# A hybrid decoder layer on one core: x in three token pieces, attention scores as three one-pass products, y split two tiles ahead

## The chip, the core and the metric

The kernel runs on one core of a Trainium2 chip. The time is the device time of one launch in microseconds; the kernel before was run three times, and the median stands for it. A separate, profiled execution left the trace that all views here come from. Engines: PE is TensorE's matrix product and PEld its weight load, DVE is VectorE, ACT is ScalarE, POOL is GpSimd, SP issues transfers.

## The reference

One decoder layer over 16 meta tokens and 1024 tokens (1040 positions), width 1024. Two mixers read the same normalised x; their outputs go through W_out, and a gated convolution FFN follows.

```python
xn = rms_norm(h, mix_pre_g[l])
proj = xn @ w_in[l]                       # z, xbc, dt, q, k, v
y_ssd = ssd_mixer(z, xbc, dt_raw, ...)
y_sb = rms_norm(stick_breaking_attention(q, k, v).reshape(Bsz, L, SB_WIDTH), sb_norm_g[l])
mix = jnp.concatenate([y_ssd, y_sb], axis=-1) @ w_out[l]
h = h + rms_norm(mix, mix_post_g[l])
# then h = h + rms_norm(ffn(rms_norm(h)))
```

The attention has 16 heads of 64. For a query t and an earlier key s the weight is beta[t,s] times the product of (1 - beta[t,j]) over the keys j between, with beta = sigmoid(q.k/8).

## The kernel before, in words

**Products in split precision.** Most float32 products are made of three one-pass products of type float32r: an operand a is split into a high part ah (a rounded) and a low part al = a - ah, and ah*bh + al*bh + ah*bl is summed in one PSUM bank. ScalarE makes the high part, GpSimd or VectorE the low part. Products of plain float32 operands appear in the trace as two records each.

**Stages.** x is normalised, transposed and split into `xh` and `xl` (L197 to L283). The SSD mixer follows (to 415 us of the trace), then the attention (415 to about 981 us), then W_out's second half with the norms, then the FFN's up and down products. W_out's first half takes the SSD output and is done inside the attention.

**Projections.** `project_steps` (L154) multiplies one 1024 x 128 weight block, split by `load_w`, with all tokens in the three chunks of `CH`: 348, 346 and 346 columns, 24 products each, into a bank of tag "mm" of which there are two. It yields after each chunk, or also half-way through one where `halves_` is set. `qkv_steps` (L353) makes q, k and v of one pair of heads p (0 to 7) so: nine steps for pair 0, fifteen for pair 1, eighteen for the others. Steps of all pairs in a row, with the transposes of v behind each pair, form `fill` (L661). Twelve of its 135 steps run in the SSD stage.

**Attention.** The loop at L897 goes through 8 pairs of heads and 8 query blocks of 128; a block is written (p,i). TensorE's order there is the program's order (L896); a planner of the framework orders the other engines, from dependencies, program order and modelled costs. Each block does in turn:

- `block_weights` (L682): scores `z` of the block against n = 16 + 128(i+1) keys, in chunks of up to 512 keys (144; 272; 400; two of 264, 328, 392, 456; three of 348, 348, 344). q and k are float32; the two heads of the pair lie on partitions 0 to 63 and 64 to 127. ScalarE takes two sigmoids of each chunk, VectorE scans each head (L704), GpSimd multiplies (L706). Scores and transposes share two double banks, tag "zz". For i = 7 the third chunk comes only after the next item.
- `run(fill, 1 + (i < 3))` (L905): one or two projection steps.
- `block_mix` (L726): the weights of an earlier block times v, `av`, in two column halves.
- `block_turn` (L710): transposes `tw` of the weights of the block two before; ScalarE copies them out as `th`.
- one more projection step (L914).

At i = 3 `edge_mix` (L750) of the pair before stands between scores and projection. From the counts of L905 and L914, pairs 1 to 5 use 19 steps each, and `fill` is used up in (6,4).

**W_out's first half.** After `fill` has ended (L915), the pool of x is closed and a pool of its own is opened in its place. `wout_steps` (L813) takes the eight 128-row blocks of W_out: the raw block (loaded ahead from (6,4), L907), the high part on ScalarE, the low part on VectorE (L828), and small products for the two halo rows (L820) into one of the two "mm" banks. Four blocks are prepared in (6,5), four in (6,6). `ssd_half` (L876) then multiplies the eight token tiles of y with W_out, two steps of 24 products per tile: one step in (6,7), in pair 7 at i = 1, 3, 5, 6, 7, and the rest behind the attention. The y of tile t+1 is loaded and split (`split_y`, L853: transfer, ScalarE, GpSimd) when tile t begins. Behind the attention its raw tile comes from the pool `est` (L961), which is opened there.

Of the kernel before, what the change touches and what calls it, by code (L numbers as in the profile page):

```python
# [8 lines left out]
F32 = mybir.dt.float32  # L9
# [22 lines left out]
CH = [(0, 348), (348, 346), (694, 346)]  # L32
# [19 lines left out]
def tile_layer(ctx: ExitStack, tc: tile.TileContext, x, meta, rows, parts,  # L52
# [101 lines left out]
    def project_steps(w, ncol, xh, xl, chunks, evac, name, halves_=False):  # L154
        hi, lo = w
        for c0, n in chunks:
            acc = psum_mm(f"pj_{name}_{c0}")
            for k in range(KB):
                if halves_ and k == KB // 2:
                    yield  # L160
                for j, (a, b) in enumerate(((hi, xh), (hi, xl), (lo, xh))):
                    mm(acc[:ncol, :n], a[:, k, :ncol], b[:, k, c0:c0 + n],
                       start=(k == 0 and j == 0), stop=(k == KB - 1 and j == 2))
# [33 lines left out]
    xh = xp.tile([P, KB, L], F32R, name="xh", tag="xh")  # L197
    xl = xp.tile([P, KB, L], F32R, name="xl", tag="xl")

    def conv_chain(b, nm, w, halves_=False):  # L200
# [5 lines left out]

        return raw, project_steps(w, P, xh, xl, CH, ev, nm, halves_)

    dtT = rp.tile([32, L + 3], F32, name="dtT", tag="rt", bufs=1)

    def dt_steps(hl):
        for c0, n in CH:
            acc = psum_mm(f"pj_dt_{c0}")
            for k in range(KB):
                for j, src in enumerate((xh, xl)):
                    mm(acc[:32, :n], hl[:, k, :], src[:, k, c0:c0 + n],
                       start=(k == 0 and j == 0), stop=(k == KB - 1 and j == 1))
# [4 lines left out]
    with tc.tile_pool(name="pre", bufs=3, side="right") as pre, \  # L222
# [46 lines left out]
        def turn_x(i):  # L269
            c0, nr = spans[i]  # L270
            tps = []
            for hf in range(2):
# [6 lines left out]
                tps.append((tp, (slice(None), slice(4 * hf, 4 * hf + 4), slice(c0, c0 + nr))))  # L279
            for tp, dst in tps:  # L280
                nc.scalar.activation(xh[dst], tp[:, :, :nr], AF.Copy)
            for tp, dst in tps:
                nc.vector.tensor_tensor(xl[dst], tp[:, :, :nr], xh[dst].bitcast(F32), op=ALU.subtract)  # L283
# [62 lines left out]
    def qkv_block(name, evac, halves_):  # L346
        w = weights_of(name)
        for i, _ in enumerate(project_steps(w, P, xh, xl, CH, evac, name, halves_)):
# [3 lines left out]

    def qkv_steps(p, post):  # L353
        q = rp.tile([P, L + 3], F32, tag="rq", name=f"q{p}", bufs=3)
        k = rp.tile([P, L], F32, tag="rk", name=f"k{p}", bufs=3)
        for dst, nm in ((q, "q"), (k, "k")):
            def ev(acc, c0, n, dst=dst):
                nc.scalar.activation(dst[:, c0:c0 + n], acc[:, :n], AF.Copy)

            yield from qkv_block(f"{nm}{p}", ev, p > 1 or (p, nm) == (1, "k"))  # L360
        vt = rp.tile([P, L], F32, tag="rt", name=f"vt{p}", bufs=1)

        def evv(acc, c0, n):
            nc.scalar.activation(vt[:, c0:c0 + n], acc[:, :n], AF.Copy)

        v = rp.tile([P, NT + 1, P], F32, tag="rv", name=f"v{p}")
        vc = rp.tile([P, P], F32, tag="vc", name=f"vc{p}")
        heads[p] = q, k, v, vc
        yield from qkv_block(f"v{p}", evv, p > 0)

        def turn_v(part):
            tp = psum_tp(f"vtp{p}_{part}")
# [5 lines left out]
        def turn_edge():  # L378
            edge = rp.tile([P, NT, NM], F32, tag="edge", name=f"edge{p}", bufs=1)
# [7 lines left out]
            nc.vector.tensor_copy(meta_k[:, p, :], k[:, 0:NM])  # L387
# [20 lines left out]
    with tc.tile_pool(name="ssd", bufs=1, side="right") as sp:  # L408
# [49 lines left out]
        def z_steps(g, b):  # L458
# [5 lines left out]
            yield from project_steps(load_w(w_z[4 * g + b], P, f"z{g}{b}"), P, xh, xl, CH, evz, f"z{g}{b}")  # L464
# [216 lines left out]

    def block_weights(p, i):  # L682
        q, k = heads[p][:2]
        nm = f"{p}_{i}"
        if i == 0:
            edges[p] = ap.tile([P, 2, NT, NM], F32, tag="cb", name=f"cb{p}", bufs=2)
            nc.gpsimd.memset(edges[p][:, :, :, NM - 1:], 0.0)
        t0, n = NM + i * P, NM + (i + 1) * P
# [4 lines left out]
        for ci, (a, w) in enumerate(chunks):  # L693
# [3 lines left out]
            for j in range(2):  # L697
                h = halves[j]
                mm(z[:, j, :w], q[h, t0:t0 + P], k[h, a:a + w], start=True, stop=True)  # L699
            nc.scalar.activation(kp[:, :, a:a + w], z[:, :, :w], AF.Sigmoid, scale=-QSCALE)  # L700
            nc.scalar.activation(bt[:, :, a:a + w], z[:, :, :w], AF.Sigmoid, scale=QSCALE)  # L701
        m = n - NM
# [110 lines left out]
    def wout_steps(pool, half, gain, res, y0, acc, raws_):  # L813
# [930 lines left out]
```

## Time and profile before

| | us |
|---|---|
| median of 3 runs | 1810.53 |
| lowest, highest | 1805.03, 1811.18 |
| profiled execution, whole | 1805.86 |
| its span, first to last instruction | 1804.2 |
| attention, from the first scores | 415.2 |
| attention, store of the last pair's output | 981.7 |

In a view of windows a row holds the stretch, its length, then for each engine the busy time and the number of records, the granted clock of TensorE (1.00 is full), the share of the transfer engines in use, and GB/s. In a timeline a row holds start, length (up to the last end of what was merged), engine, line, operation, output and inputs, shapes and count; records of TensorE overlap, so that the time of one is read from one start to the next. In the groups, the number behind the bar is the busy time, then the mean of one in ns, then the idle time of the engine ahead of them with what ended it. In a view of waits: total, times, longest.

### The profile page before, as it was taken

The numbers are of one execution on the slowest core, as the hardware profiler recorded it, in microseconds if no ns is written. First come the engines' busy times: TensorE is split into PE (matmuls) and PEld (weight loads), VectorE is DVE, ScalarE is ACT, GpSimd is POOL, SyncE is SP. The second block draws the span as 40 slices with busy tenths as digits, with TensorE's granted clock in tenths as the row PEclk, the third lists the DMA queues.
The fourth block names the chain that finished last, engine by engine and source line by source line (L and its number), as shares of the span: only waits on it lengthen the run. The fifth ranks groups of instructions, "written<-read, shape, count | busy, mean of one in ns | idle before, by whom it ended". The sixth has DMA issues, their size and how long they took to land. (4 is left out here: it accounts for less than half of the span.)

```text
span 1804.2 us, 27314 instructions
## 1 busy us (share of the span) xinstructions
PE 1732.4 (96%) x10942; PEld 1487.3 (82%) x10942; DVE 1061.6 (59%) x1125; ACT 830.8 (46%) x1373; POOL 867.8 (48%) x615
## 2 busy tenths in 40 slices
PE   6999999999999999999799899899999999999997
PEld 6899889888888888886567588888999988888886
DVE  5651964873463454355741256666766666657988
ACT  5423553645565565566653333543333333244444
POOL 4223753676555564554751223277777776600001
PEclk9999999999999999999999899999999999999999
DMA  4133333231011011012212545222333332196344
GB/s 157 48 97 106 106 118 107 71 94 36 24 37 48 24 36 37 24 48 71 72 42 95 193 140 164 82 88 88 117 100 106 101 105 88 64 320 227 95 123 158
DMA packets 90547, 173.96 MB, mean 96 GB/s; under 512 B 10698, under 2 KB 35818, under 8 KB 90420
## 3 DMA queue, kind: packets, MB, share of 16 engines
q1 hardware_dynamic: 90420, 172.21, 30.0%
q8 instruction: 86, 1.41, 0.3%
q14 instruction: 41, 0.34, 0.1%
HBM read 122.39 MB, written 49.79 MB: 95 GB/s over the span
## 5 line engine op out<-in xcount | busy, mean ns | idle before, releaser
L704 DVE TENSOR_TENSOR_SCAN kp<-kp,hold 128x272 f32<-128x272 f32 (+7 forms) x128 | 207.8, 1665 | 193.5 <-ACT kp L700 103.2
L706 POOL TENSOR_TENSOR bt<-bt,kp 128x256 f32<-128x256 f32 (+7 forms) x128 | 214.7, 1695 | 188.9 <-DVE kp L704 132.7
L1109 POOL TENSOR_TENSOR wl<-wr,wh 128x1024 fp32r<-128x1024 f32 x44 | 110.7, 2524 | 40.7 <-ACT wh L1108 40.7
L1557 PE MATMUL dn<-dl,dh 128*128 128x512 f32 x308 | 119.9, 389 | 0.1
L1557 PE MATMUL dn<-dh 128*128 128x512 f32 x308 | 119.9, 389 | 0.0
L1557 PE MATMUL dn<-dh,dl 128*128 128x512 f32 x308 | 119.8, 389 | 0.0
L1603 POOL TENSOR_TENSOR fms<-fms,nhalf 128x1 f32<-128x1 f32 x8 | 8.5, 1060 | 225.7 <-DMA ar<-fda 186.0
L700 ACT ACTIVATE kp<-z 128x288 f32<-128x288 f32 (+6 forms) x112 | 82.8, 739 | 56.7 <-PE z L699 33.0
L1486 ACT ACTIVATE dh<-ar 128x512 fp32r<-128x512 f32 x77 | 48.7, 632 | 111.3 <-PE dn L1557 90.7
L699 PE MATMUL z<-k,q 64*128 64x144 f32 (+6 forms) x448 | 86.9, 487 | 13.3 <-ACT bt L701 6.0
L1108 ACT ACTIVATE wh<-wr 128x1024 fp32r<-128x1024 f32 x44 | 46.6, 1060 | 114.7 <-PE fX L1166 68.3
L1238 DVE SCALAR_TENSOR_TENSOR ga<-gr,pp,ga 128x1024 f32<-128x1024 f32 x44 | 71.4, 1622 | 34.8 <-ACT ga L1231 34.0
L722 ACT ACTIVATE th<-tw 128x1024 f32<-128x1024 f32 (+2 forms) x96 | 74.7, 813 | 34.1 <-PE tw L720 32.2
L701 ACT ACTIVATE bt<-z 128x288 f32<-128x288 f32 (+6 forms) x112 | 83.1, 742 | 0.0
L720 PE MATMUL tw<-ident,bt 128*128 128x128 f32 x576 | 77.6, 280 | 3.8 <-issue 2.8
L734 PEld LDWEIGHTS av<-th,v 128*64 128x64 f32 x1152 | 62.6, 138 | 18.9 <-issue 17.9
L734 PE MATMUL av<-th,v 128*64 128x128 f32 x1152 | 78.0, 281 | 0.0
L1487 DVE TENSOR_TENSOR dl<-ar,dh 128x512 fp32r<-128x512 f32 x77 | 53.2, 691 | 41.7 <-ACT dh L1486 41.7
L720 PEld LDWEIGHTS tw<-ident,bt 128*128 128x128 f32 x576 | 62.1, 141 | 15.5 <-issue 12.9
L699 PEld LDWEIGHTS z<-k,q 64*128 64x128 f32 x448 | 36.7, 186 | 41.8 <-issue 18.5
L1557 PEld LDWEIGHTS dn<-dl,dh 128*128 128x128 f32 x308 | 57.8, 188 | 12.5 <-DVE dl L1487 0.4
L1557 PEld LDWEIGHTS dn<-dh 128*128 128x128 f32 x308 | 57.8, 188 | 12.4 <-ACT dh L1486 0.3
(550 smaller groups left out, 5752.6 us busy)
## 6 DMA issues: line engine op xcount, KB each, us to landing
wr<-in_w_up SPq DMA_DIRECT2D x44, 512.0 KB
fds<-ga SPq DMA_DIRECT2D x44, 256.0 KB
b<-in_w_down SPq DMA_DIRECT2D x44, 256.0 KB
ar<-fds SPq DMA_DIRECT2D x44, 256.0 KB
fda<-ga SPq DMA_DIRECT2D x33, 256.0 KB
ar<-fda SPq DMA_DIRECT2D x33, 256.0 KB
yk<-yd SPq DMA_DIRECT2D x16, 512.0 KB
zd<-zt SPq DMA_DIRECT2D x8, 520.0 KB
```

The costliest lines, as they stand in the source:

```text
L699: mm(z[:, j, :w], q[h, t0:t0 + P], k[h, a:a + w], start=True, stop=True)
L700: nc.scalar.activation(kp[:, :, a:a + w], z[:, :, :w], AF.Sigmoid, scale=-QSCALE)
L701: nc.scalar.activation(bt[:, :, a:a + w], z[:, :, :w], AF.Sigmoid, scale=QSCALE)
L704: nc.vector.tensor_tensor_scan(kp[:, j][:, ::-1], kp[:, j][:, ::-1], hold[:, L - n:L][:, ::-1], 0.0, op0=ALU.mult, op1=ALU.max)
L706: nc.gpsimd.tensor_tensor(bt[:, j, 0:m], bt[:, j, 0:m], kp[:, j, 1:m + 1], op=ALU.mult)
L720: nc.tensor.transpose(tw[:, j, b, :], bt[:, j, c0:c0 + P], ident)
L722: nc.scalar.activation(th[:, :, :nb, :], tw[:, :, :nb, :], AF.Copy)
L734: mm(av[halves[j], :], v[:, kb, halves[j]], th[:, j, b, :], start=kb == 0, stop=kb == i)
L1109: nc.gpsimd.tensor_tensor(l, raw, h.bitcast(F32), op=ALU.subtract)
L1238: nc.vector.scalar_tensor_tensor(v, self.g[jj][:, :, i:i + 256], fconv_w[:, j, i:i + 1], v, op0=ALU.mult, op1=ALU.add)
L1487: sub(lo[:, k], raw, hi[:, k].bitcast(F32), op=ALU.subtract)
L1557: mm(banks[t], u[:, 0, c], v[:, 1, :], start=(p == 0 and i == 0), stop=(p == NPR - 1 and i == 2))
```

## The change

x is kept as three tiles (`xs`), one for each chunk of tokens (400, 384, 256 columns), each with its high and low part. The projections of pair 7 go through the chunks one by one, q, k and v of each, so that a tile of x is free after its chunk. W_out's first half is put into these tiles: three blocks in the first, three in the second, two in the third (`third_slots`), one block for each attention block from (6,2) to (7,1), with its raw loads issued there. The halo accumulator is taken at (6,2).

The scores become three float32r products for each head. k is split where it leaves PSUM (`kh` on ScalarE, `kl` on VectorE), q block by block, one block ahead (`split_q`, on VectorE). The values `av` come straight behind the scores. One projection step per block goes (`FILL`), so that pairs 2 to 6 use 17 steps. The products of W_out's first half run one step per block from (7,2).

`ssd_half` splits the y of tile t+2 when tile t begins; two are split ahead of the first.

```diff
-CH = [(0, 348), (348, 346), (694, 346)]
+CH = [(0, 400), (400, 384), (784, 256)]
...
-                for j, (a, b) in enumerate(((hi, xh), (hi, xl), (lo, xh))):
-                    mm(acc[:ncol, :n], a[:, k, :ncol], b[:, k, c0:c0 + n],
+                for j, (a, b) in enumerate(((hi, 0), (hi, 1), (lo, 0))):
+                    mm(acc[:ncol, :n], a[:, k, :ncol], xs[c0][:, b, k, :n],
...
-    xh = xp.tile([P, KB, L], F32R, name="xh", tag="xh")
-    xl = xp.tile([P, KB, L], F32R, name="xl", tag="xl")
+    def x_third(c0, name):
+        n = dict(CH)[c0]
+        return xp.tile([P, 2, KB, n], F32R, name=name, tag=f"x{c0}")
+
+    xs = {c0: x_third(c0, f"xs{c0}") for c0, _ in CH}
...
+        def ev_k(acc, c0, n):
+            if c0 == 0:
+                low_k()
+            kl = later["kl"]
+            nc.scalar.activation(kh[:, c0:c0 + n], acc[:, :n], AF.Copy)
+            nc.vector.tensor_tensor(kl[:, c0:c0 + n], acc[:, :n], kh[:, c0:c0 + n].bitcast(F32), op=ALU.subtract)
...
+        names = [(f"q{p}", ev_q), (f"k{p}", ev_k), (f"v{p}", ev_v)]
+        if p < 7:
+            for nm, ev in names:
+                yield from qkv_block(nm, ev, p > 1 or (p == 1 and nm != "q1"))
+        else:
+            for c in CH:
+                for j, (nm, ev) in enumerate(names):
+                    w = weights_of(nm)
+                    for i, _ in enumerate(project_steps(w, P, [c], ev, nm, True)):
+                        if i == 1 and c[0] == 0:
+                            weights_of(nm, 1)
+                        yield
+                left[0] += 1
...
-            nc.vector.tensor_copy(meta_k[:, p, :], k[:, 0:NM])
+            nc.vector.tensor_tensor(meta_k[:, p, :], kh[:, 0:NM].bitcast(F32), kl[:, 0:NM].bitcast(F32), op=ALU.add)
...
+    def split_q(p, i):
+        q = heads[p][0][:, NM + i * P:NM + (i + 1) * P]
+        qh = rp.tile([P, P], F32R, tag="qh", name=f"qh{p}_{i}", bufs=2)
+        ql = rp.tile([P, P], F32R, tag="ql", name=f"ql{p}_{i}", bufs=2)
+        nc.vector.tensor_copy(qh, q)
+        nc.vector.tensor_tensor(ql, q, qh.bitcast(F32), op=ALU.subtract)
+        qsplit[p, i] = qh, ql
...
-            for j in range(2):
-                h = halves[j]
-                mm(z[:, j, :w], q[h, t0:t0 + P], k[h, a:a + w], start=True, stop=True)
+            for s_, (u, r) in enumerate(((qh, kh), (ql, kh), (qh, kl))):
+                for h, j in zip(halves, range(2)):
+                    mm(z[:, j, :w], u[h, :], r[h, a:a + w], start=s_ == 0, stop=s_ == 2)
...
+        nxt = (p, i + 1) if i < NT - 1 else (p + 1, 0)
+        if nxt[0] in heads:
+            split_q(*nxt)
...
+    def third_slots():
+        free = []
+
+        def slots(k, nm):
+            if not free:
+                c0 = CH[k // 3][0]
+                flat = x_third(c0, f"wo{nm}{c0}").rearrange("p a b c -> p (a b c)")
+                free.extend(flat[:, o * D:(o + 1) * D] for o in range(2 * dict(CH)[c0] // P))
+            return free.pop(0), free.pop(0)
+
+        return slots
...
-            if t < NT:
-                ys.append(split_y(wp, 0, t + 1, ("whi", "wlo", WB)))
             y = ys.pop(0)
+            if t < NT - 1:
+                ys.append(split_y(wp, 0, t + 2, ("whi", "wlo", WB)))
...
+    FILL = (3, 2, 1, 1, 1, 1, 1, 0)
+    STAGE = {(6, 2): 1, (6, 3): 2, (6, 4): 3, (6, 5): 4, (6, 6): 5, (6, 7): 6, (7, 0): 7, (7, 1): 8}
...
             next(block, None)
+            if mix:
+                block_mix(*mix.pop(0))
             if p > 0 and i == 3:
                 edge_mix(p - 1, edge)
-            run(fill, 1 + (i < 3))
...
+            run(fill, 1 + (i < FILL[p]))
             run(block)
-            if mix:
-                block_mix(*mix.pop(0))
             if len(turn) > 2:
                 mix.append(block_turn(*turn.pop(0)))
             run(fill, int(p > 0 or i > 3))
...
+            if left[0] and wsteps is None:
+                wres = []
+                halo = psum_mm("halo0")
+                wsteps = wout_steps(third_slots(), 0, ssd_g, wres, halo_y(ap, 0, ssd_g), halo, [])
+            for _ in range(2):
+                if wsteps and len(wres) < min(8, 3 * left[0], STAGE.get((p, i), 0)):
+                    run(wsteps, 1)
+            if wsteps and first is None and len(wres) == 8:
+                run(wsteps)
+                halo_store(ap, 0, halo)
+                ys1 = [split_y(wp, 0, t, ("whi", "wlo", WB)) for t in (1, 2)]
+                first = ssd_half(wres, ys1)
+            elif first:
+                run(first, 1)
```

More of the change, by code (lines that the diff above doesn't have):

```diff
@@ L152, in load_w, with project_steps @@
         return hi, lo
[L154 removed]
+    def project_steps(w, ncol, chunks, evac, name, halves_=False):
         hi, lo = w
@@ L351, in qkv_block @@
             yield
+    left = [0]
     def qkv_steps(p, post):
         q = rp.tile([P, L + 3], F32, tag="rq", name=f"q{p}", bufs=3)
[L355 to L369, printed above, removed]
+        kh = rp.tile([P, L], F32R, tag="rk", name=f"kh{p}", bufs=3)
+        later, vt_ = {}, []
+        def values():
+            v = rp.tile([P, NT + 1, P], F32, tag="rv", name=f"v{p}")
+            vc = rp.tile([P, P], F32, tag="vc", name=f"vc{p}")
+            heads[p][2:] = [v, vc]
@@ L371, in turn_v @@
         def turn_v(part):
+            if part == 0:
+                values()
+            v, vt = heads[p][2], vt_[0]
             tp = psum_tp(f"vtp{p}_{part}")
@@ L981, in tile_layer @@
         nc.sync.dma_start(out=mts[-1], in_=mixd[t - 1])
-    halo_store(w1pool, 1, halo)
+    halo_store(est, 1, halo)
     wo1.close()
+    xpool.close()
     token_rstd(r_sb, op, "b")
```

65 lines of the change are left out of this document (34 added, 31 removed).

## The prediction, as made before the result

> **What bounds the kernel now.** I read the page first (busy shares, then the groups), next the windows by stage, then the timeline of TensorE around one attention block, then the waits of TensorE in the two windows where it idles.
>
> ```profile
> span 1804.2 us, 27314 instructions
> PE 1732.4 (96%) x10942; PEld 1487.3 (82%) x10942; DVE 1061.6 (59%) x1125; ACT 830.8 (46%) x1373; POOL 867.8 (48%) x615
> core 0: us, PE busy (x) PEld busy (x) DVE busy (x) ACT busy (x) POOL busy (x), PEclk, DMA share, GB/s
> 603.90:672.00 68.10, 67.81 (x518) 57.22 (x517) 30.66 (x24) 39.49 (x66) 38.86 (x30) 1.00 0.13 34
> 740.10:808.20 68.10, 67.81 (x518) 57.23 (x517) 30.90 (x26) 38.28 (x64) 35.67 (x29) 1.00 0.13 40
> 837.10:880.50 43.40, 31.03 (x214) 18.22 (x213) 41.19 (x24) 36.65 (x58) 33.06 (x16) 0.96 0.23 74
> 880.50:938.00 57.50, 51.39 (x365) 38.10 (x364) 23.72 (x21) 29.43 (x50) 38.89 (x33) 0.97 0.22 66
> 994.00:1011.00 17.00, 9.13 (x37) 4.48 (x28) 4.39 (x4) 8.16 (x11) 7.15 (x3) 0.70 0.68 223
> ```
>
> TensorE is busy 96% of the span. A pair of heads in the middle of the attention (603.9 to 672.0, 740.1 to 808.2) lasts 68.1 us with TensorE at 67.81, while VectorE, ScalarE and GpSimd are at 31 to 39: there only less TensorE work shortens anything. Three windows differ. In 837.1 to 880.5 (pair 6 from its fourth block on) TensorE idles 12.4 us and VectorE is busy 41.19 of 43.40, so VectorE is the bound. In 880.5 to 938.0 (pair 7) TensorE idles 6.1 us. In 994 to 1011, just behind the attention, it idles 7.9 us and its granted clock is 0.70. All times below are against the profiled execution: 1805.86 us, the span and 1.7 us around it. It lies 4.7 us under the median of the runs shown, 1810.53, whose lowest is 1805.03.
>
> **1. Scores.** For each chunk of keys two heads run side by side, each in two recorded passes of float32.
>
> ```profile
> 759.72 0.94 PE L699 MATMUL z<-k,q 64*128 64x400 f32 x4
> 760.60 0.43 PE L162 MATMUL pj_v<-xh,wh_v 128*128 128x346 f32 x1
> 760.86 0.32 PE L162 MATMUL pj_v<-xl,wh_v 128*128 128x346 f32 x1
> 761.02 0.32 PE L162 MATMUL pj_v<-xh,wl_v 128*128 128x346 f32 x1
> 776.20 1.38 PE L699 MATMUL z<-k,q 64*128 64x328 f32 x8
> 777.50 0.43 PE L162 MATMUL pj_q<-xh,wh_q 128*128 128x348 f32 x1
> 1199.63 0.28 PE L1166 MATMUL fY<-b22h,wh 128*128 128x258 f32 x1
> 1202.98 0.28 PE L1166 MATMUL fX<-t4l,ah 128*128 128x258 f32 x1
> 1640.00:1680.00 40.00, 40.00 (x178) 33.11 (x177) 1.00 0.43 138
> ```
>
> What counts is from one start to the next. Four records of 400 columns (two passes of a pair) take 760.60 - 759.72 = 0.88 us, eight of 328 (four passes) 1.30. With c per column and pass and s for entering and leaving, 800c + s = 0.88 and 1312c + s = 1.30: c = 0.82 ns, s = 0.22 us. The key chunks of a pair of heads sum to 4736 columns in 14 chunks, so its scores now take 2 x 4736 x 0.82 = 7.8 us.
>
> One-pass products stand in the other rows: between the two of 258 columns at 1199.63 and 1202.98 lie 28 steps, 0.120 us each; those of 512 columns (down projection) take 40.00/178 = 0.225. So 0.415 ns per column and 0.0125 us per product. Three per chunk make 3 x (0.415 x 4736 + 14 x 12.5) = 6.4 us: 1.4 less per pair, 10.8 for eight. The 144-column chunk may be held by its weight loads (up to 0.1 us each, eight times). I take **-10**. This supposes that one-pass products of two heads also run side by side, which no row shows for this type (rival 2): -10.8 is one end, +41 the other.
>
> **2. Fewer changes of the array's shape.** The shape is the pair before the operand sizes: 64*128, 128*64, 128*128.
>
> ```profile
> 764.35 0.32 PE L162 MATMUL pj_v<-xh,wl_v 128*128 128x346 f32 x1
> 764.60 1.97 PE L734 MATMUL av<-th,v 128*64 128x128 f32 x32
> 766.49 0.44 PE L720 MATMUL tw<-ident,bt 128*128 128x128 f32 x2
> 880.54 0.52 PE L699 MATMUL z<-k,q 64*128 64x144 f32 x4
> 880.99 1.53 PE L734 MATMUL av<-th,v 128*64 128x128 f32 x24
> 779.37 0.32 PE L162 MATMUL pj_q<-xh,wl_q 128*128 128x348 f32 x1
> 779.52 0.60 PE L375 MATMUL vtp<-ident,vt 128*128 128x128 f32 x4
> ```
>
> A projection followed by another starts it 0.16 us later (760.86 to 761.02), followed by values 0.25 (764.35 to 764.60): +0.09. Values straight behind scores cost what a projection there costs: 880.54 to 880.99 is 0.45 = 2 x 144 x 0.82 ns + 0.21. Projection to transpose costs nothing (0.15). A block now runs scores, projection, values, transposes, projection; with the values put behind the scores it runs scores, values, projection, transposes, projection. Gone are the drain into the values and the transposes' own start (values of 32 records take 1.89 us for 16 x 0.106, so 0.19 is lost there, half of it kept): 0.12 us a block. In the fourth block the edge product, of the values' shape, falls next to them and saves about 0.2 more. 47 such blocks x 0.12 + 6 x 0.2 = 6.8; between 4 and 8.5, I take **-6.5**.
>
> **3. Pairs 6 and 7.** By the counts of steps, the projections now end in (6,4). Then W_out's first half is prepared within (6,4) to (6,6), and its products run in only six of the last nine blocks. The change takes 2 half blocks of projection from each of pairs 2 to 5 (moved, not gained) and spreads pair 7's over pair 6 to (7,1), prepares one W_out block per step from (6,2) to (7,1), and runs a product in each block from (7,2).
>
> ```profile
> PE z L699 <- ACT bt L701: 5.0, 2, 4.7
> PE tw L720 <- issue: 2.8, 5, 0.8
> PE z L699 <- DVE thc L746: 2.6, 2, 2.3
> PE mo L870 <- POOL yl L860: 2.2, 1, 2.2
> L704 DVE TENSOR_TENSOR_SCAN kp<-kp,hold 128x528 f32<-128x528 f32 (+4 forms) x10 | 22.4, 2281 | 0.5 <-ACT kp L700 0.5
> L828 DVE SCALAR_TENSOR_TENSOR wola<-wora,pp,woha 128x1024 fp32r<-128x1024 f32 x6 | 13.3, 2247 | 0.2 <-ACT woha L827 0.2
> 985.76 1.38 SPq L807 DMA_DIRECT2D worb<-in_w_out  x3
> 989.59 1.15 ACT L827 ACTIVATE wohb<-worb,pp 128x1024 fp32r<-128x1024 f32 x1 [1.53 <-DMA worb<-in_w_out]
> ```
>
> Idle in both windows: 12.4 + 6.1 = 18.5 us, about 2 more through the clock (0.96, 0.97). In 837 to 881 W_out's splits (the six of this row 13.3 us, two more beside them) stand among ten scans (22.4); spread over eight blocks of 8 us they leave VectorE room. What stays: TensorE's wait for the first split of y, whose load needs the raw slots of W_out's last blocks (a transfer of 3.8, ScalarE about 1.1 as in the row above, GpSimd's subtraction behind it, with about 4 us of other TensorE work ahead; the same wait is 2.2 now): 3.5 us. The meta steps and waits for banks of scores: 2.5. New: the halo accumulator holds one of two projection banks from (6,2) to (7,1), so each projection chunk waits until the one before is out of its bank; for k that is now VectorE behind two scans (2.3 us each), some 3 us at (6,4) and at (6,7): 6 with the small ones. 20.5 - 12 = 8.5; between 0 (VectorE still the bound) and 17. I take **-8**.
>
> The raw loads of W_out lose their head start: they go through two slots, each freed by a halo product one block earlier (8 us), and the first of three such 512 KB transfers issued at 985.76 was in use at 989.59, 3.8 us later, so that block hides them.
>
> **4. y two tiles ahead.**
>
> ```profile
> PE mo L870 <- ACT yh L859: 3.9, 1, 3.9
> PE mo L870 <- POOL yl L860: 2.1, 1, 2.1
> PE halo L820 <- DMA worb<-in_w_out: 1.9, 1, 1.9
> 1007.49 0.63 PE L870 MATMUL mo<-woha,yh 128*128 128x512 f32 x1
> 1007.92 0.63 PE L870 MATMUL mo<-woha,yl 128*128 128x512 f32 x1
> ```
>
> Behind the attention the seventh y is loaded only once est's space is free, and TensorE waits 3.9 + 2.1 us for its two parts; the products behind it start 0.43 us apart instead of 0.23, about ten of them: 2 us of clock. Two tiles ahead, this y is split during the attention, and the eighth has two steps (11 us) of cover. The 1.9 us for the W_out block stays. 6 + 2 = 8 at most, 2 if the store queue or the raw slots hold it again; I take **-7**.
>
> **5. What is added.** k's low part on VectorE (24), q's split (64 x 2), a sum for meta_k.
>
> ```profile
> L283 DVE TENSOR_TENSOR xl<-xtp,xh 128x512 fp32r<-128x512 f32 (+1 forms) x18 | 10.6, 628 | 1.6 <-ACT xh L281 1.5
> L380 DVE COPY edge<-vt 128x112 f32<-128x112 f32 x1 | 0.3, 270 | 3.4 <-ACT vt L364 3.4
> ```
>
> A subtraction from a bank took 0.63 us at 512 columns, so about 0.5 at 346; a copy of 112 columns 0.27. Per pair 3 x 0.5 + 16 x 0.27 = 5.8 us on VectorE, beside 31 of 68: hidden in pairs 0 to 5. Behind a k subtraction that waits for two scans stands the bank; with two banks the next chunk (24 x 0.16 = 3.8 us) and the block's other products cover it. q's split is issued a block ahead, before that block's scans. Without that cover, 3 us for each of 21 chunks: 0 to +8, I take **+2**. The thirds themselves (400, 384, 256 columns) sum to the same 1040 and the same number of products: 0; the first chunk needs the same four tiles of x as before.
>
> Sum: -10 - 6.5 - 8 - 7 + 2 = -29.5: 1805.86 - 29.5 = 1776.4. Runs lie up to 5 us above that profiled one; I give **1778**.
>
> **Rivals.** *1: VectorE stays the bound in pairs 6 and 7* and the bank shared with the halo costs more than the spreading gives: part 3 gives 0, part 5 costs 8: 1778 + 8 + 6 = 1792, up to 1800. For it: VectorE at 41.19 of 43.40 and k's evacuation behind scans. Against: W_out's splits now lie in over twice the time. *2, slower: the one-pass products of the two heads do not run side by side.* Each chunk then takes six one after another: 6 x (0.415 x 4736 + 175) = 12.8 us per pair of heads instead of 7.8, so +41 instead of -10: 1778 + 51 = 1829. It decides from 4 us per pair of heads lost, where parts 2 to 4 are used up. For it: no row has this type in this shape. Against: float32 passes in this shape run in pairs (s + 800c above), and shape and type are set apart. *3: the loads of the third product are not hidden.*
>
> ```profile
> L699 PEld LDWEIGHTS z<-k,q 64*128 64x128 f32 x448 | 36.7, 186 | 41.8 <-issue 18.5 <-ACT bt L701 7.3 <-ACT th L722 5.9
> ```
>
> If every load in the same half of the array stood open, 112 chunks x 3 x 0.186 = 62 us would come on top: 1840. Passes of 328 columns now follow at 0.27 us with a new load each and no gap, which speaks against it. The Trainium skill, "TensorE: Matmul & The Clock Gate", section "Part 3: Packing small matmuls — row/col tiling", has that rule: loads overlap running products only where their row group differs. By that rule this kernel's consecutive projections (0.16 us with a load each) could not run as they do; the trace disagrees with its strict reading, so it gets little.
>
> **How the numbers follow.** Forecast 0.71 (its own range 1765 to 1790: the ends of parts 2 to 5). Rival 1 0.14, rival 2 0.08, rival 3 0.03; 0.04 that nearly all idle goes, 1763. The range 1763 to 1800 holds forecast, rival 1 and the last: 0.89 before misjudged terms, about 0.8 with them. About 0.5% is what a measurement tells from no change: 1801.5 to 1819.6 around 1810.53. Faster: 0.71 + 0.11 + 0.04 = 0.86; same: 0.03, the upper end of rival 1; slower: rivals 2 and 3, 0.11.
>
> **What would show it.** Right: score records x6 or x12, 400 columns from scores to values in about 0.75 us instead of 0.88; a middle pair near 68.1 - 3.8 (two half blocks) - 2.4 = 62 us; the two idle windows together under 13 us; no wait for yh behind the attention. Wrong: score records of a pair that start more than 0.1 us apart; TensorE waits released by k's subtraction, or for W_out loads, over 10 us in sum; VectorE over 90% busy in pair 6.

## The result, and the profile after

| | before | after |
|---|---|---|
| median, us | 1810.16 | 1779.11 |
| lowest, highest (4 runs each) | 1805.03, 1811.18 | 1777.51, 1779.84 |
| profiled execution | 1805.86 | 1779.84 |
| its span | 1804.2 | 1778.1 |

The ratio of after to before is 0.984, with a 95% interval of [0.9824, 0.9856]: 1.6% faster by it; the two medians lie 31 us apart. The prediction was 1778. Beside the experiments below the kernel before was run again, with medians from 1806.2 to 1807.3; against these the change gains 27 to 28 us. The change itself was not run again there, so that a difference of 1 or 2 us from its 1779.11 is not shown.

The head of the page, and the windows by stage. The borders of the windows are the first score products of the pairs, as they were for before (530.5 is pair 2, 592.6 pair 3, 717.7 pair 5, 780.3 pair 6, 853.8 pair 7; 807.6 is block (6,3), where the window of before from 837.1 starts too); 1003.8 is the first product `mo` of W_out's second half.

```profile
span 1778.1 us, 27927 instructions
PE 1718.2 (97%) x11166; PEld 1510.3 (85%) x11166; DVE 1123.8 (63%) x1277; ACT 827.2 (47%) x1373; POOL 868.8 (49%) x615
```

```profile
core 0: us, PE busy (x) PEld busy (x) DVE busy (x) ACT busy (x) POOL busy (x), PEclk, DMA share, GB/s
592.60:655.30 62.70, 61.19 (x516) 54.97 (x515) 40.36 (x42) 37.48 (x63) 36.77 (x30) 1.00 0.12 35
717.70:780.30 62.60, 61.29 (x522) 55.45 (x521) 39.60 (x43) 37.20 (x63) 35.65 (x29) 1.00 0.10 32
807.60:853.80 46.20, 40.34 (x315) 33.05 (x314) 32.88 (x31) 28.38 (x45) 23.70 (x15) 0.93 0.19 58
853.80:921.10 67.30, 60.44 (x443) 48.55 (x439) 35.53 (x38) 38.00 (x66) 43.16 (x34) 0.92 0.30 96
977.00:1003.80 26.80, 26.44 (x134) 19.96 (x130) 5.43 (x8) 11.68 (x18) 7.21 (x4) 1.00 0.69 222
```

A middle pair went from 68.1 to 62.6 us (62.4 on average; about 62 had been forecast). VectorE has 40 us in it instead of 31 and is still far from the bound. In pair 6 from its fourth block on VectorE fell from 41.19 of 43.40 to 32.88 of 46.20, so it is no longer the bound there; yet TensorE idles 5.9 us in this window, and 6.9 in the next (12.4 and 6.1 before). Behind the attention the idle time and the slow clock are gone (26.44 of 26.80 at 1.00). The waits of TensorE from pair 6 to 1004 name what is left (total, times, longest):

```profile
PE pj_v L162 <- DVE kl L382: 3.8, 1, 3.8
PE mo L936 <- POOL yl L926: 3.4, 1, 3.4
PE tw L772 <- ACT bt L750: 1.8, 4, 0.8
PE mo L936 <- ACT yh L925: 1.6, 1, 1.6
```

Two waits stand out: one for the low part of k in (6,4), and one for the first y in (7,2), 3.4 + 1.6 us. Both had been forecast; the next table shows what each edit does to the stages.

**The stages in all kernels** (us, from the traces; the columns: first scores; pairs 0 and 1 together; mean of pairs 2 to 5; pair 6; pair 7 up to the first product of W_out's second half; the rest). The labels are those of the experiments below.

| kernel | first scores | 0, 1 | 2 to 5 | 6 | 7 | rest |
|---|---|---|---|---|---|---|
| before | 415.2 | 120.6 | 68.1 | 72.3 | 152.1 | 771.6 |
| after | 412.6 | 117.9 | 62.4 | 73.5 | 150.0 | 774.3 |
| e_f32 | 410.5 | 119.0 | 63.4 | 69.4 | 152.1 | 773.9 |
| e_late | 413.0 | 116.7 | 62.8 | 72.5 | 153.0 | 774.0 |
| e_packed | 411.3 | 119.3 | 67.0 | 70.8 | 139.5 | 774.1 |
| e_unpaired | 411.1 | 118.0 | 62.5 | 72.9 | 150.1 | 774.0 |
| e_oney | 412.7 | 117.9 | 62.4 | 72.9 | 161.9 | 772.1 |
| e_pack_one | 411.1 | 119.3 | 67.0 | 71.1 | 154.9 | 771.9 |
| e_ahead | 417.9 | 120.6 | 68.1 | 80.2 | 139.3 | 774.6 |
| e_chunks | 414.3 | 122.1 | 68.1 | 71.5 | 152.6 | 771.7 |
| m_halo | 413.8 | 116.3 | 62.4 | 67.9 | 150.9 | 773.8 |
| m_raw | 414.3 | 116.3 | 62.4 | 72.8 | 143.9 | 772.3 |
| m_both | 413.6 | 116.3 | 62.4 | 67.9 | 145.8 | 772.4 |
| m_both_f32 | 413.3 | 118.8 | 63.5 | 72.7 | 143.7 | 772.6 |

### The profile page after: what moved, and what is told of

Same layout as the page of the kernel before. It is cut to its first block, busy times and chain, and to the rows that moved or that the text cites. A ratio compares the mean times of both kernels' runs of the same rounds, so it can differ in the third digit from the quotient of the medians.

```text
span 1778.1 us, 27927 instructions
## 1 busy us (share of the span) xinstructions
PE 1718.2 (97%) x11166; PEld 1510.3 (85%) x11166; DVE 1123.8 (63%) x1277; ACT 827.2 (47%) x1373; POOL 868.8 (49%) x615
## 5 line engine op out<-in xcount | busy, mean ns | idle before, releaser
L756 DVE TENSOR_TENSOR_SCAN kp<-kp,hold 128x272 f32<-128x272 f32 (+7 forms) x128 | 185.6, 1490 | 30.7 <-ACT kp L749 22.9
L162 PE MATMUL pj_v<-xs,wh_v 128*128 128x400 f32 (+2 forms) x384 | 97.5, 342 | 3.8 <-DVE kl L382 3.8
L162 PE MATMUL pj_k<-xs,wh_k 128*128 128x400 f32 (+2 forms) x384 | 94.7, 333 | 0.7 <-ACT q L375 0.7
L724 DVE CAST qh<-q 128x128 fp32r<-128x128 f32 x64 | 38.5, 603 | 89.9 <-PE z L748 89.6
L162 PE MATMUL pj_q<-xs,wh_q 128*128 128x400 f32 (+2 forms) x384 | 95.2, 335 | 0.0
L162 PE MATMUL pj_X<-xs,wh_X 128*128 128x400 f32 (+2 forms) x384 | 92.8, 330 | 0.2 <-ACT craw_X L208 0.2
L162 PE MATMUL pj_z<-xs,wh_z 128*128 128x400 f32 (+2 forms) x384 | 92.2, 328 | 0.0
L936 PE MATMUL mo<-woa,yh 128*128 128x512 f32 x256 | 83.8, 400 | 1.6 <-ACT yh L925 1.6
```

Source lines behind the costliest of these rows:

```text
L162: mm(acc[:ncol, :n], a[:, k, :ncol], xs[c0][:, b, k, :n], start=(k == 0 and j == 0), stop=(k == KB - 1 and j == 2))
L756: nc.vector.tensor_tensor_scan(kp[:, j][:, ::-1], kp[:, j][:, ::-1], hold[:, L - n:L][:, ::-1], 0.0, op0=ALU.mult, op1=ALU.max)
L936: mm(acc, u[:, k, :], v[:, cs], start=(k == 0 and j == 0), stop=(k == 7 and j == 2))
```

## The experiments

The theory is the prediction's sum: scores, order of the values, pacing of pairs 6 and 7, and y two ahead each carry their own part. The rivals are that one of them carries nearly all, or that parts are lost again to new waits. Each time is a median, each ratio against the kernel before, with its 95% interval. Kernels e_f32 to e_unpaired, m_raw, m_halo and e_oney are the changed kernel with one edit; e_ahead and e_chunks are the kernel before with one edit.

**e_f32: scores in float32 again.** No low part of k, no split of q.

```diff
-            for s_, (u, r) in enumerate(((qh, kh), (ql, kh), (qh, kl))):
-                for h, j in zip(halves, range(2)):
-                    mm(z[:, j, :w], u[h, :], r[h, a:a + w], start=s_ == 0, stop=s_ == 2)
+            for h, j in zip(halves, range(2)):
+                mm(z[:, j, :w], q[h, t0:t0 + P], k[h, a:a + w], start=True, stop=True)
...
```

> The changed kernel with the scores back in plain float32: k and q are not split, one float32 product per head and chunk (two records), nothing else undone. Terms of the prediction: 10 us more, 1789, and the stall behind k's low part at (6,4) (3.8 us, plus a dip of the clock) gone, so 1784 to 1789. Rival (the splits of q, 0.6 us each on VectorE in the new trace, eat the gain by making the scores or transposes wait): 1779 or less.

Measured: 1780.21, 0.9859 [0.9844, 0.9874], 1.1 us over the change; the two intervals overlap, so that the sum shows no difference. The windows of a middle pair and of pair 6:

```profile
592.90:656.40 63.50, 62.60 (x488) 52.94 (x487) 30.16 (x23) 37.33 (x63) 39.25 (x30) 1.00 0.11 34
783.30:852.70 69.40, 66.99 (x516) 54.62 (x515) 41.32 (x31) 42.25 (x68) 37.87 (x28) 1.00 0.14 46
```

The middle pair is 1.0 us longer than with one-pass products, pair 7 is 2.1 longer; but pair 6 is 4.1 shorter, at a clock of 1.00: without a low part of k there is no wait for it. So the products gain, and the split loses most of it again at one place. m_both_f32 below takes the place away. VectorE at 30.16 instead of 40 buys little in the middle pairs: the waits of TensorE for VectorE in pairs 2 to 5, first of after, then of this kernel, differ by 1.3 us in four pairs:

```profile
PE z L748 <- DVE thc L798: 1.6, 3, 0.8
PE z L748 <- DVE meta_k L423: 0.9, 1, 0.9
```

```profile
PE z L742 <- DVE thc L789: 0.9, 3, 0.3
PE z L742 <- DVE meta_k L420: 0.3, 1, 0.3
```

**e_late: values in their old place**, behind the projection.

```diff
-            if mix:
-                block_mix(*mix.pop(0))
             if p > 0 and i == 3:
                 edge_mix(p - 1, edge)
...
             run(block)
+            if mix:
+                block_mix(*mix.pop(0))
```

> The changed kernel with the values back behind the projection, as before. Terms of the prediction: 6.5 us more, 1785.5. Rival, from the new trace: the time that a middle pair of heads needs beyond its products hardly fell (about 7 us before and after, though 8 changes of shape fewer), so the place of the values is worth 0 to 2 us: 1779 to 1781.

Measured: 1781.92, 0.9869 [0.9854, 0.9883]: 2.8 us over the change, between the 6.5 of the theory and the rival's 0 to 2; the two intervals overlap a little. By the stages a middle pair grows by 0.4 and pair 7 by 3.0. TensorE's waits of the transposes in pairs 2 to 5, first of after, then of this kernel (the waits for `thc` and `meta_k` are the same in both):

```profile
PE tw L772 <- ACT bt L750: 2.2, 4, 0.9
```

```profile
PE tw L772 <- ACT bt L750: 0.3, 1, 0.3
```

With the values late, the transposes hardly wait for the weights (0.3 us in four pairs instead of 2.2): the values were part of the cover of ScalarE's sigmoids. Per pair the saved shape changes so give 0.9 us, of which the new wait takes 0.5 and 0.4 stays.

**e_packed: W_out's first half packed into (6,5) and (6,6) as before**, its raw blocks loaded ahead, its products in the old blocks, 19 projection steps per pair; y stays two ahead.

```diff
-    FILL = (3, 2, 1, 1, 1, 1, 1, 0)
-    STAGE = {(6, 2): 1, (6, 3): 2, (6, 4): 3, (6, 5): 4, (6, 6): 5, (6, 7): 6, (7, 0): 7, (7, 1): 8}
+    FILL = (3, 3, 3, 3, 3, 3, 3, 3)
+    STAGE = {(6, 5): 4, (6, 6): 8}
...
```

> The changed kernel with the old pacing: projection steps per block as before, W_out's first half prepared in (6,5) and (6,6) behind all projections from raw blocks loaded ahead, its products in the old blocks. Thirds, scores, place of the values and y two ahead stay. Terms of the prediction: the spreading was worth 8 us, 1787, with VectorE again over 90% busy in that stretch. Rival (the stall behind k at (6,4) and the longer wait for the first y gave it all back): 1779.

Measured: 1785.48, 0.9889 [0.9871, 0.9907]: the pacing is worth 6.4 us. Steps move from pairs 6 and 7 back to the middle pairs (67.0 each, pair 7 139.5); from the first scores to the first product of W_out's second half it is 597.6 us instead of 591.2. Pair 6 from block (6,3) on:

```profile
824.60:869.40 44.80, 31.39 (x238) 21.41 (x237) 39.28 (x31) 32.86 (x54) 33.85 (x18) 0.89 0.28 92
```

VectorE is busy 88% of it, a little under the 90% expected, and TensorE idles 13.4 us, about as in the kernel before; 5.8 of them it waits for the low part of the first y. What each part of the pacing is worth (steps moved, blocks of W_out spread, its products one in a block) isn't told apart.

**e_unpaired: the products of one head, then those of the other.**

```diff
-            for s_, (u, r) in enumerate(((qh, kh), (ql, kh), (qh, kl))):
-                for h, j in zip(halves, range(2)):
+            for h, j in zip(halves, range(2)):
+                for s_, (u, r) in enumerate(((qh, kh), (ql, kh), (qh, kl))):
```

> The changed kernel with the three products of the first head of a pair issued ahead of those of the second, so that they cannot run side by side except where one head follows the other. If products of the two heads run side by side in the changed kernel, this loses most of that: rival 2's price, 51 us by the prediction, less where the last of one and the first of the other overlap (a third): 30 to 51 us more, 1809 to 1830. If the side by side were not there or did not matter: 1779.

Measured: 1778.77, 0.985 [0.983, 0.987], no difference (two runs). Its trace still shows the first products of the two heads 10 ns apart (median of 112 pairs; 3 ns in after), though two others stand between them in the program. So the order written out for the heads isn't what makes them run together; whether TensorE or a step between program and chip puts them side by side, the traces don't tell.

**e_ahead: the kernel before, with only y two ahead.**

```diff
-            if t < NT:
-                ys.append(split_y(wp, 0, t + 1, ("whi", "wlo", WB)))
             y = ys.pop(0)
+            if t < NT - 1:
+                ys.append(split_y(wp, 0, t + 2, ("whi", "wlo", WB)))
...
-                ys1 = [split_y(wp, 0, 1, ("whi", "wlo", WB))]
+                ys1 = [split_y(wp, 0, t, ("whi", "wlo", WB)) for t in (1, 2)]
```

> The kernel before with one part of the change alone: y of W_out's first half split two tiles ahead. Prediction's term: 7 us less, 1803 against 1810, with no wait for yh behind the attention and full clock there. Rival (the store queue or the raw slots hold the seventh y again): under 2 us less.

Measured: 1805.97, 0.9987 [0.9975, 0.9999]: 1.3 us. The waits behind the attention (3.9 + 2.1) are gone, and most of the gain is given back in pair 6 (another 3.0 us in the rest). Windows of pair 6 and of the stretch behind it, of the kernel before and then of this one:

```profile
808.20:880.50 72.30, 59.93 (x452) 44.27 (x451) 49.29 (x31) 46.94 (x76) 43.14 (x28) 0.98 0.18 59
880.50:1032.60 152.10, 136.75 (x844) 102.76 (x843) 41.92 (x40) 65.63 (x100) 60.19 (x44) 0.96 0.31 102
```

```profile
810.80:891.00 80.20, 62.27 (x452) 46.15 (x452) 48.87 (x31) 47.24 (x76) 48.81 (x31) 0.91 0.21 67
891.00:1030.30 139.30, 131.83 (x843) 99.93 (x843) 37.86 (x40) 65.22 (x99) 54.11 (x41) 1.00 0.31 104
```

The last stretch is 12.8 us shorter, pair 6 is 7.9 longer. The timeline of ScalarE in block (6,7) says why:

```profile
873.27 0.74 ACT L701 ACTIVATE bt<-z 128x696 f32<-128x696 f32 x1
881.15 1.06 ACT L859 ACTIVATE yh<-yk 128x1024 fp32r<-128x1024 f32 x1 [7.13 <-DMA yk<-yd]
882.11 0.73 ACT L700 ACTIVATE kp<-z 128x688 f32<-128x688 f32 x1
```

The split of the third y is issued there. Its transfer is issued only at 877.73, when GpSimd's subtraction for the first y (from 874.36, 3.34 us) has freed a raw slot. ScalarE waits 7.13 us for the transfer; behind it in its order stand the sigmoids of the block's last chunk, and TensorE waits for them:

```profile
883.52 1.11 PE L720 MATMUL tw<-ident,bt 128*128 128x128 f32 x4 [6.84 <-ACT bt L701]
```

**e_chunks: the kernel before, with only the new sizes.**

```diff
-CH = [(0, 348), (348, 346), (694, 346)]
+CH = [(0, 400), (400, 384), (784, 256)]
```

> The kernel before with the chunk sizes alone: 400, 384 and 256 columns in place of 348, 346 and 346; x still in two tiles. Prediction: 0, 1810. Rival, from the two traces: the scores begin 2.6 us earlier in the changed kernel although nothing else touches what stands ahead of them, so the sizes gain about 2.6 us there by covering waits of the SSD stage: 1806 to 1808, with the first scores at about 412.6 in the trace.

Measured: 1802.53, 0.9974 [0.9964, 0.9984]: 4.7 us, outside the interval of no change, and more than the rival's 2 to 4. Its profiled execution, the slowest of its ten runs, does not show the gain (span 1804.5, before 1804.2), but it shows a place. The waits of TensorE in the SSD stage (50 us to the first scores), of before, then of this kernel:

```profile
PE tt_B L431 <- DVE bn L427: 2.9, 1, 2.9
PE yt L627 <- DVE yo L613: 2.7, 4, 1.2
PE cb L571 <- ACT ct L420: 2.0, 1, 2.0
```

```profile
PE cb L571 <- ACT ct L420: 2.4, 1, 2.4
PE pz_ea L534 <- DVE s L522: 1.5, 1, 1.5
PE yt L627 <- DVE yo L613: 0.6, 1, 0.6
```

The wait of 2.9 us for `bn` is gone and that for `yo` is shorter. In this trace the scores start only 0.9 us earlier. But all twelve traces with the new sizes start the scores between 410.5 and 414.3, on average at 412.6; the two with the old ones at 415.2 and 417.9. By an estimate from these starts (412.6 in after against 415.2, and the two averages, 412.6 against 416.6) two to four us of the change come from there; with only two traces of the old sizes this isn't firm, and the rest of the 4.7 isn't located.

**m_raw: the last two raw blocks of W_out in slots of the y parts.**

```diff
-            wr = raws_.pop(0) if raws_ else raw_w(half, k, None)
+            wr = raws_.pop(0) if raws_ else raw_w(half, k, wp_f32(("whi", "wlo")[k - 6], f"wora{k}") if k > 5 else None)
```

> The changed kernel with the raw blocks 6 and 7 of W_out's first half loaded into two free weight slots instead of the two raw slots, so that the raw slots are free for the first two tiles of y one block earlier. The new trace shows 5.0 us of waiting for the first y in (7,2), and the clock dips behind it: if the raw slots are what holds this load, 5 to 7 us less, 1772 to 1774. If the store queue or the planner's order holds it: 1779.

Measured: 1771.57, 0.9797 [0.9776, 0.9818]: 7.5 us less than the change. No wait for yh or yl is left: the raw slots of W_out's last blocks held the first y.

**m_halo: the halo accumulator taken at (6,4)**, where the projections need fewer banks, with W_out's first blocks two at a time.

```diff
-    STAGE = {(6, 2): 1, (6, 3): 2, (6, 4): 3, (6, 5): 4, (6, 6): 5, (6, 7): 6, (7, 0): 7, (7, 1): 8}
+    STAGE = {(6, 4): 2, (6, 5): 4, (6, 6): 5, (6, 7): 6, (7, 0): 7, (7, 1): 8}
...
-            if left[0] and wsteps is None:
+            if (p, i) == (6, 4):
```

> The changed kernel with W_out's first half begun two blocks later, in (6,4), two blocks of it each in (6,4) and (6,5), so that the halo accumulator takes its bank only when the second k chunk of pair 7 has left its own. The new trace shows 3.8 us of waiting on k's low part in (6,4), with a dip of the clock behind it: if the shared bank is the cause, 4 to 6 us less, 1773 to 1775. Rival (VectorE is behind anyway and the wait comes elsewhere, or the raw loads come late): 1779 or more.

Measured: 1774.05, 0.9809 [0.9792, 0.9826]: 5.1 us less; pair 6 falls to 67.9 and no wait for k's low part is left. What that wait was made of, in the timelines of VectorE and TensorE of after:

```profile
819.16 2.94 DVE L756 TENSOR_TENSOR_SCAN kp<-kp,hold 128x656 f32<-128x656 f32 x2 [1.09 <-ACT kp L749]
822.01 2.27 DVE L879 SCALAR_TENSOR_TENSOR woa<-wor,pp,woa 128x1024 fp32r<-128x1024 f32 x1
824.21 0.55 DVE L382 TENSOR_TENSOR kl<-pj_k,kh 128x384 fp32r<-128x384 f32 x1
```

```profile
824.81 1.01 PE L162 MATMUL pj_v<-xs,wh_v 128*128 128x384 f32 x2 [3.80 <-DVE kl L382]
825.94 0.85 PE L162 MATMUL pj_v<-xs,wh_v 128*128 128x384 f32 x2
826.90 0.85 PE L162 MATMUL pj_v<-xs,wh_v 128*128 128x384 f32 x2
```

The subtraction of k stands behind two scans and a split of W_out, 5.2 us of VectorE, and the only free projection bank waits for it. Behind the 3.8 us three products take 0.96 us (825.94 to 826.90) instead of 0.54 (818.61 to 819.15 in the same block): the granted clock is 0.50 from 824.8 to 829.0, which costs another 2.5 us or so. The Trainium skill, "TensorE: Matmul & The Clock Gate", section "Part 1: The HAM clock gate", states half the clock after an idle window of about 3.4 us, and as much busy time to regain it; these rows agree in kind: 3.8 us of idle, then half the clock; the slow products last 5 us here (824.8 to 829.8).

**m_both: both mends together.**

> The changed kernel with both edits that shortened it one at a time: the raw blocks 6 and 7 of W_out's first half take slots of the y parts instead of the raw slots (alone 1771.57), and the halo accumulator is taken at (6,4) instead of (6,2) (alone 1774.05). Theory: TensorE waits 3.8 us for k's low part in (6,4) and 5.0 us for the first y in (7,2); the two waits are 40 us apart on different queues, so the gains 7.5 and 5.1 add: 1766 to 1768, and neither wait is in the trace. Rival: both are paid back at the same place, since the blocks of W_out that start later push the first y later: 1770 to 1773, with a wait for y of 2 to 4 us in (7,2) again.

Measured: **1767.18**, 0.9777 [0.9763, 0.979]: 11.9 us less than the change, 40 less than the kernel before beside it. Of the 12.6 that the two gave alone nearly all stays, and neither wait is in its trace.

**m_both_f32: the kernel with both mends, scores in float32.** The edit of e_f32 on m_both.

> The kernel of the run before it with scores in plain float32, without the low part of k and the split of q. With the shared bank still there, float32 scores were 1 us slower only. Theory: the one-pass products gain 1.0 us per pair in the middle pairs and 2 in the last, some 7 us in all, and lost 4 of them to the wait for k's low part; here no such wait is left, so float32 costs the full 6 to 8 us: 1773 to 1776. Rival: one-pass scores gain nothing in sum, because q's split on VectorE delays the scans everywhere: within 2 us of the run before it, 1766 to 1769.

Measured: 1776.33, 0.9825 [0.9808, 0.9842]: 9.2 us over m_both. The windows of pair 6, of m_both and then of this kernel:

```profile
779.60:847.50 67.90, 65.50 (x546) 56.55 (x545) 47.59 (x50) 42.42 (x68) 37.40 (x28) 1.00 0.19 63
```

```profile
786.00:858.70 72.70, 68.58 (x516) 55.69 (x515) 41.54 (x31) 42.57 (x68) 37.80 (x28) 0.98 0.19 59
```

Pairs 0 to 5 together are 6.7 us longer, 1.1 a pair. Pair 6 is 4.8 longer and pair 7 is 2.1 shorter: each kernel has one wait of TensorE for the copies `th` there, this one in pair 6 (2.1 us), m_both in pair 7 (1.8), with the slower clock in the same pair. Taken together the two are 2.7 longer. The sum is: with the shared bank out of the way the one-pass products are worth about 9 us, and with it 1.

**e_oney: the changed kernel with y one tile ahead.** The edit of e_ahead, the other way.

> The changed kernel with the y of W_out's first half split one tile ahead again (one split ahead of the first). Theory: with W_out spread out, two ahead is worth what the wait behind the attention was, 6 us and its clock, 7 to 9 us, while in the kernel before it was worth 1.3 only because the second y then stood among the packed W_out blocks of pair 6 (that pair grew by 8 us): 1786 to 1789, with waits for yh and yl behind the attention. Rival: two ahead is worth little here too, since the spread products end later and cover the load: 1779 to 1782, no such wait.

Measured: 1788.42, 0.9895 [0.9881, 0.9909]: 9.3 us over the change. Its waits from 853 to 1015:

```profile
PE mo L936 <- POOL yl L926: 5.6, 2, 3.5
PE mo L936 <- ACT yh L925: 5.3, 2, 3.8
PE halo L872 <- DMA worb<-in_w_out: 2.1, 1, 2.1
```

Against the change (3.4 and 1.6, and none for a block of W_out) 6 us of waits for y are back and 2.1 for W_out. The stretch from pair 7 on is 11.9 us longer, and 2.2 come back behind it.

**e_pack_one: packed and one ahead**, both edits on the changed kernel.

> The changed kernel with both parts of the pacing undone: W_out's first half packed into (6,5) and (6,6) as before (alone 1785.48, 6.4 over the change) and its y split one tile ahead (alone 1788.42, 9.3 over). Theory A, the two are separate: 1779 + 6.4 + 9.3 = 1795, with the 6 us of waits for yh and yl behind the attention. Theory B, they need each other, as in the kernel before, where two ahead gained 1.3 us because the second y stood in front of pair 6's sigmoids on ScalarE: 1785 to 1788, and pair 6 shorter than with two ahead. What is left to the 1807 of before, 12 or 20 us, is then the share of scores, order of the values and sizes together.

Measured: 1796.42 (1790.12 to 1801.52), 0.9931 [0.9911, 0.9952]: the two add (A), as far as the spread of the runs lets it be told. So y two ahead is worth some 11 us beside packed W_out blocks as well, and packing alone was not what spoiled it in the kernel before. In e_packed the third y's copy on ScalarE starts only at 868.33, after the block's last sigmoids at 854.66; in e_ahead it stood in front of them. Where that copy falls in ScalarE's order is the difference that the traces show; no run moves the copy alone.

## Why the prediction was right, point by point

The time came out 1.1 us from the forecast, and 29.5 of gain against 31.0 measured (26.0 between the two profiled executions). The terms were less exact than the sum, and that their errors partly cancel is luck: scores and values gave some 10 us less than forecast, y two ahead 2 more, and the sizes several us that had been put at nothing.

| term | predicted | measured |
|---|---|---|
| scores, with the additions on VectorE | -10 + 2 | -1.1 in the change (not clear of noise); -9.2 once k's low part holds no bank |
| values behind scores | -6.5 | -2.8 |
| pairs 6 and 7 | -8 | -6.4 |
| y two ahead | -7 | -9.3 in the change; -1.3 alone |
| chunk sizes | 0 | -4.7 alone, 2 to 4 of it located |

- **Scores.** The timeline of a block of 400 columns in a middle pair:

```profile
672.98 0.45 PE L748 MATMUL z<-kh,qh 64*128 64x400 f32 x2
673.27 0.34 PE L748 MATMUL z<-kh,ql 64*128 64x400 f32 x2
673.45 0.34 PE L748 MATMUL z<-kl,qh 64*128 64x400 f32 x2
673.72 0.55 PE L786 MATMUL av<-th,v 128*64 128x128 f32 x6
```

From scores to values it is 0.74 us, forecast 0.75; two heads run side by side, so rivals 2 and 3 fell. The first of the three takes 0.29 instead of 0.18, part of the 0.22 us that the prediction had for entering and leaving. Chunk by chunk the gain is as priced: two of 328 columns take 1.10 us instead of 1.30, two of 392 take 1.26 instead of 1.52, and only the chunk of 144 is longer, 0.49 instead of 0.45. Over a middle pair that comes to about the 1.4 us forecast; 1.0 to 1.1 are left because TensorE waits 0.3 us a pair longer for `thc` and `meta_k` (at e_f32). The mechanism was right, and the gain was hidden in the change by the wait that part 3 had priced: a term of one part paid for the new wait in another.
- **Fewer shape changes.** Mis-sized: -6.5 against 2.8. The changes do fall (from 33 in a pair of e_late to 25), and are worth the 0.9 us a pair that was forecast; but the step left out that the values had covered the wait of the transposes for the sigmoids, 0.5 us per pair. The prediction did not ask what the values had been covering.
- **Pairs 6 and 7.** Right in kind and place. Predicted: 3 us at (6,4) for the bank, 3.5 for the first y. Measured: 3.8 and 5.0, each with a slow clock behind it, so that without them 5.1 and 7.5 go (2.0 of the 7.5 in the rest, at the clock told of below). The wait forecast for (6,7) did not come. VectorE, at 32.88 of 46.20, was under the 90% that rival 1 needed.
- **y two ahead.** Mis-sized in the change, 9.3 against 7 and above the bound of 8: the wait for the W_out block, which the prediction let stay, went too (2.1 in e_oney, none in after). The bound "2 if the raw slots hold it again" is what the kernel before shows, 1.3, with ScalarE's wait ahead of the sigmoids as the mechanism; the prediction gave no place for it.
- **Additions.** Cover held except for the 0.3 us a pair above and the wait at (6,4). q's split costs VectorE more than the copy of 112 columns that it was priced by. The groups of VectorE from 412 to 853:

```profile
L725 DVE TENSOR_TENSOR ql<-q,qh 128x128 fp32r<-128x128 f32 x56 | 37.5, 669 | 1.9
L724 DVE CAST qh<-q 128x128 fp32r<-128x128 f32 x56 | 33.2, 593 | 85.9 <-PE z L748 85.6
L382 DVE TENSOR_TENSOR kl<-pj_k,kh 128x400 fp32r<-128x400 f32 (+2 forms) x21 | 10.8, 512 | 31.2 <-ACT kh L381 31.2
```

q's two instructions take 0.59 and 0.67 us instead of 0.27; k's, which reads PSUM, the 0.5 that was estimated.
- **Sizes.** "0" was wrong: they change no product count, but two waits in the SSD stage change with them, presumably through the length of the evacuations. This term was never looked up in the stage where it acts; it covered the shortfall of the values.
- **Not foreseen:** behind the attention 2.7 us are given back (771.6 to 774.3). e_ahead shows it too (774.6), e_oney (772.1) and m_raw (772.3) do not: of the fourteen kernels those with y two ahead have it, except the three with m_raw's edit, and none with y one ahead. 1.6 of it is the clock at the start of W_out's second half, in windows of after, then of m_raw:

```profile
1003.80:1010.00 6.20, 6.16 (x20) 4.99 (x21) 1.09 (x1) 0.00 (x0) 2.77 (x1) 0.72 0.70 239
```

```profile
997.10:1003.30 6.20, 6.16 (x27) 5.13 (x28) 1.42 (x2) 0.00 (x0) 2.77 (x1) 1.00 0.70 239
```

In after the products of 512 columns start 0.43 us apart for the first 3.5 us, in m_raw 0.23 from the first on. In both, the same 18 small products (2.07 us) and a wait of 0.4 us stand ahead of them; why the clock falls in the one and not in the other the traces don't show. Another 0.8 is a longer wait ahead of the transposes of the next stage (0.9 to 1.7), of which m_raw has 0.7 as well.

**Do the parts close the sum?** From before (1806.9 beside that run) to e_pack_one, which keeps scores, values' place and sizes, it is 10.5 us; the pacing and y two ahead then bring 17.3 to 1779.1. Predicted were 14.5 and 15. The first part doesn't close: measured apart, scores without the shared bank, the values' place and the sizes come to 16.7 (9.2, 2.8, 4.7). The runs of e_pack_one spread over 11 us; in its pair 6 TensorE waits 5.8 us for the low part of the first y where before has 2.2, and the granted clock is 0.93 there and 0.91 behind it, where before has 0.98 and 0.96. How much of the 6 us lies there isn't settled. So the schedule brought most of the gain; the arithmetic of the scores brought its 9 us only once its own wait was gone.

## What to carry to other kernels

A part that gains and a part that stalls can share one cause: undo a part both with and without the stall that it brings, as e_f32 and m_both_f32 do, before its worth is read. A load that is issued further ahead must be followed through every in-order engine that touches it: the copy that waits for it holds all that stands behind. Two small mends, found by reading which buffer the late instruction waits for, gave 12 us more, over a third of what the whole change gave. A cost taken from a row must come from an instruction of the same kind: same shape of access, beside the same engines.

## What the runs showed of the hardware that was not expected

- Short VectorE copies beside GpSimd: of the 64 of line 724, the 32 that overlap no GpSimd instruction take 0.225 us on average, the other 32 take 0.98, the longest 1.96. Each of the 24 that take over 0.25 us ends 0.08 to 0.09 us after a GpSimd instruction ends. At the end of a middle pair of after:

```profile
591.15 2.30 DVE L756 TENSOR_TENSOR_SCAN kp<-kp,hold 128x1040 f32<-128x1040 f32 x1
593.37 1.96 DVE L724 CAST qh<-q 128x128 fp32r<-128x128 f32 x1
595.36 1.99 DVE L725 TENSOR_TENSOR ql<-q,qh 128x128 fp32r<-128x128 f32 x1
```

The same two take 0.23 and 0.29 us where GpSimd rests. The Trainium skill, "SBUF — State Buffer", section "SBUF: two separate sides", describes a port pair that VectorE and GpSimd share, as a lock that one of them holds for a whole instruction; the ends of these copies agree. The row that the prediction costed by was not held, though it ran beside GpSimd: the copy of 112 columns, read in seven pieces of 16, takes 0.27 us at 709.51 of before, inside a GpSimd instruction that runs from 709.25 to 710.34. It was not of the kind that is held. One that is stood in the groups of before from 700 to 760, a copy of two columns:

```profile
L386 DVE COPY meta_q<-q 64x2 f32<-64x2 f32 x2 | 2.5, 1239 | 0.0
```

- One-pass products of two heads in the two halves of the array started nanoseconds apart whichever order the program gave them: the first two of a chunk 3 ns apart by the median with the heads in turn, 10 ns with one head ahead of the other (e_unpaired).
